# A streaming-encoder trunk on one core: entry in two row halves, half squares ahead of the last row tiles, weight sums first, and the up projections' stores on GpSimd's queue

## The chip, the core and the metric

The program runs on one core of a Trainium2 chip. The metric is the device time of one execution in microseconds (us). The core's engines are TensorE (PE, matrix products; its weight loads show as PEld), VectorE (DVE), ScalarE (ACT), GpSimd (POOL) and SyncE (SP, which only issues transfers here). Each engine takes its instructions in order. ACT and POOL can issue transfers too, and then the issue stands in their own order.

## The reference, cut to what matters

Two layers over 1024 rows of width 1024, all in float32. Layer 0 mixes with a gated short convolution, layer 1 with attention; both end in a squared-ReLU MLP of width 4096. Ahead of each mixer and MLP stands a norm, scaled and shifted by vectors that are made from the conditioning vector c.

```python
for l in range(DEPTH):
    mod = c_act @ ada_w[l] + ada_b[l]
    sh_m, sc_m, g_m, sh_f, sc_f, g_f = split(mod, 6)
    h = rmsnorm(x, norm_g[l, 0]) * (1 + sc_m) + sh_m
    y = short_conv_mixer(h, ...) if l < 1 else mla_mixer(h, ..., shared_kv(x, ...))
    x = x + g_m * rmsnorm(y, norm_g[l, 1])
    h = rmsnorm(x, norm_g[l, 2]) * (1 + sc_f) + sh_f
    y = square(relu(h @ mlp_up_w[l])) @ mlp_down_w[l]
    x = x + g_f * rmsnorm(y, norm_g[l, 3])

def short_conv_mixer(h, w_in, w_conv, b_conv, w_out):
    b_gate, c_gate, xh = split(h @ w_in, 3)
    return (b_gate * (causal_conv3(c_gate * xh, w_conv) + b_conv)) @ w_out
```

## The kernel before

The eight row tiles of 128 rows form two row halves (half 0, half 1), and the width of 1024 is eight blocks k of 128. Every float32 number is split into a high and a low part of a shorter type, and a product is three matmuls of 128 x 512 (low by high, high by high, high by low). Large products save one part in eight by seven products of sums of quarters (the names t1 to t4 and s in code and trace).

The stages in order: the **entry** (`conv_phase`: x is normed, scaled and transposed into k blocks, and the first two column blocks m=0, 1 of the convolution's input projection are made), three **triples** (the other column blocks in pairs, the convolution beside them), **down** (the convolution's output projection), the **first pairs** and the **up projection** of layer 0 (`mlp_up`, 16 pairs of column blocks; each pair's seven sums are stored to the DRAM arrays `ha`), **down_pairs** (reads `ha`, multiplies with the down weights, and at its end adds the residual row by row: the `Seam`), the latents, attention, and the same again for layer 1's MLP.

In the **entry**, pass 1 makes m=0 for both row halves, half 1 two k's behind (`LAG`); pass 2 makes m=1 with weights that are loaded again, 128 x 3 x 128 for each k. For each k, `ada` loads 128 columns each of shift and scale weights in four transfers, and DVE sums their eight 128 x 256 parts times c (`av`, L1006 and L1008); PE sums these over the partitions (L1010), ACT scales the transposed rows with the result (L1024), DVE makes the low part (L1025). The vectors' rows (norm gains, biases) are loaded by eight issues on ACT's queue ahead of ACT's first work.

In **down_pairs** the last product (number 2) leaves its last four k groups to the end and finishes them row tile by row tile (tiles 4 to 7). Each tile goes through `Seam.tile`: squares of the half that was ready before (L346), the add of the last half (L792), squares of it (L283), a root, the residual (L373), and where another stage follows, squares of the new row (L283), its scaling (L323) and a store. `seam.front` and `seam.back` interleave the next stage's h (`h_steps`: transposes on PE L482, ACT L485, DVE L491).

In the **up projection**, `pair_sums` makes the sums and splits of a pair's weights (L525 to L535) and `all_pairs` orders the products. `store` leaves the pair's row results, and `sums` (L1233 to L1238) makes seven stored operands of 128 x 512 and stores them, seven transfers of 256 KB, on ACT's queue. Row tiles come from a pool of eight; a pair takes four. A tile is free again when its stores have landed.

Within each engine most instructions stand in an order that a list scheduler made from the program's dependencies; what is written under `pinned` keeps the order of the code.

## Time and profile before

| | us |
|---|---|
| median of three runs | 2132.92 (2132.76 to 2133.66) |
| the profiled execution | 2132.76 |
| its span, first to last instruction | 2131.0 |
| entry, to the first product of the triples | 0 to 117.4 |
| layer 0: triples, down, first pairs, up | 117.4 to about 710 |
| layer 0: down_pairs, last tile's residual | to about 1033 |
| latents, attention, output projection, first pairs | to about 1536 |
| layer 1: up, down_pairs | to 2131 |

The mean granted clock of PE is 0.992 of full speed. The page's rows give an engine's busy time; a row of the timeline gives start, duration, engine, line, operation with its operands, how many were put together, and in brackets the idle time before it with the engine that ended it. A row of the windows gives start and end, length, then busy time and count of each engine, the granted clock, the DMA engines' share and GB/s. A row of the waits gives who waited for whom, the sum, how often, and the longest.

### The profile page before, as it was taken

The numbers are of one execution on the slowest core, as the hardware profiler recorded it, in microseconds if no ns is written. First come the engines' busy times: TensorE is split into PE (matmuls) and PEld (weight loads), VectorE is DVE, ScalarE is ACT, GpSimd is POOL, SyncE is SP. The second block draws the span as 40 slices with busy tenths as digits, with TensorE's granted clock in tenths as the row PEclk, the third lists the DMA queues.
The fourth block names the chain that finished last, engine by engine and source line by source line (L and its number), as shares of the span: only waits on it lengthen the run. The fifth ranks groups of instructions, "written<-read, shape, count | busy, mean of one in ns | idle before, by whom it ended". The sixth has DMA issues, their size and how long they took to land.

```text
span 2131.0 us, 25054 instructions
## 1 busy us (share of the span) xinstructions
PE 2054.8 (96%) x9438; PEld 1686.4 (79%) x9438; DVE 1553.8 (73%) x2100; ACT 1082.5 (51%) x1545; POOL 5.6 (0%) x13
## 2 busy tenths in 40 slices
PE   4999999999999999999899999999999999999998
PEld 3788878878888788888677788878878888888886
DVE  6877777886665579977688887758976765566577
ACT  4533354744454444455665565556745444544343
POOL 0000000000000000000000000000000000000000
PEclk9999999999999999999999999999999999999999
DMA  7344455355653889656223331135354653774255
GB/s 227 113 148 143 135 197 160 107 187 169 203 172 113 297 285 320 209 168 197 80 70 117 96 94 35 60 115 181 94 194 154 212 168 124 262 257 158 97 172 176
DMA packets 251166, 344.46 MB, mean 162 GB/s; under 512 B 19269, under 2 KB 142498, under 8 KB 251046
## 3 DMA queue, kind: packets, MB, share of 16 engines
q1 hardware_dynamic: 208840, 253.81, 37.9%
q10 hardware_dynamic: 42206, 89.06, 11.2%
q8 instruction: 74, 1.21, 0.2%
q14 instruction: 46, 0.38, 0.1%
HBM read 258.94 MB, written 83.89 MB: 161 GB/s over the span
## 4 chain that ended last, share of the span: by engine, by line
PE 78%; DVE 10%; ACT 5%; DMA 4%; issue 2%; SPq 0%; ACTq 0%; DVEq 0%
PE one L168 40%; PE mm L168 20%; PE big L168 7%; PE tp L168 6%; PE big L1471 2%; DMA raw<-ha 2%; DVE ring L172 1%; PE tp L1497 1%; ACT slot L1321 1%; DVE acc L198 1%; ACT junk L283 1%; ACT ring L171 1%; PE tp L421 1%; DVE raw L373 0%; DMA raw<-in_ada_w_dram 0%
## 5 line engine op out<-in xcount | busy, mean ns | idle before, releaser
L168 PE MATMUL one<-slot,uphi 128*128 128x512 f32 x1208 | 372.1, 389 | 0.0
L168 PE MATMUL one<-ring,ring 128*128 128x512 f32 x1152 | 262.9, 389 | 2.3 <-DVE ring L172 2.3
L168 PEld LDWEIGHTS one<-slot,uphi 128*128 128x128 f32 x1208 | 226.8, 188 | 47.2 <-issue 0.5
L168 PEld LDWEIGHTS one<-ring,ring 128*128 128x128 f32 x1152 | 215.9, 188 | 48.3 <-ACT ring L171 3.1
L168 PE MATMUL one<-slot,uplo 128*128 128x512 f32 x604 | 237.4, 393 | 5.2 <-DVE y L604 3.1
L172 DVE TENSOR_TENSOR uplo<-raw,uphi 128x1024 fp32r<-128x1024 f32 x129 | 157.6, 1222 | 85.5 <-ACT uphi L171 85.3
L172 DVE TENSOR_TENSOR ring<-raw,ring 128x1024 fp32r<-128x1024 f32 x144 | 174.2, 1219 | 59.0 <-ACT ring L171 58.6
L171 ACT ACTIVATE ring<-raw 128x1024 fp32r<-128x1024 f32 x144 | 149.4, 1052 | 120.0 <-DMA raw<-ha 76.6
L168 PE MATMUL mm<-ring,ring 128*128 128x512 f32 x768 | 185.1, 390 | 1.5 <-DVE ring L172 1.0
L168 PE MATMUL tp<-ring,ring 128*128 128x512 f32 x768 | 183.9, 389 | 0.0
L171 ACT ACTIVATE uphi<-raw 128x1024 fp32r<-128x1024 f32 x129 | 136.0, 1057 | 88.7 <-DVE raw L526 27.7
L168 PEld LDWEIGHTS mm<-ring,ring 128*128 128x128 f32 x768 | 143.6, 188 | 32.3 <-DVE ring L172 1.8
L168 PEld LDWEIGHTS tp<-ring,ring 128*128 128x128 f32 x768 | 144.1, 188 | 29.8
L171 ACT ACTIVATE ring<-w 128x1024 fp32r<-128x1024 f32 x80 | 84.7, 1059 | 158.8 <-PE tp L168 87.4
L172 DVE TENSOR_TENSOR ring<-w,ring 128x1024 fp32r<-128x1024 f32 x80 | 97.6, 1220 | 74.1 <-ACT ring L171 73.1
L198 DVE SCALAR_TENSOR_TENSOR acc<-raw,csil,acc 128x1024 f32<-128x1024 f32 x88 | 112.4, 1277 | 44.0 <-DMA raw<-in_ada_w_dram 39.3
L168 PEld LDWEIGHTS one<-slot,uplo 128*128 128x128 f32 x604 | 113.4, 188 | 32.4 <-DVE y L604 4.8
L168 PE MATMUL one<-slot,s 128*128 128x512 f32 x468 | 114.7, 395 | 6.3 <-DVE s L172 6.1
L168 PE MATMUL mm<-slot,uphi 128*128 128x512 f32 x360 | 110.9, 389 | 0.0
L168 PEld LDWEIGHTS one<-slot,s 128*128 128x128 f32 x468 | 88.6, 190 | 26.9 <-DVE s L172 7.4
L168 PE MATMUL one<-q,uphi 128*128 128x512 f32 x312 | 96.0, 389 | 0.0
L168 PE MATMUL big<-slot,slot 128*128 128x512 f32 x384 | 93.8, 391 | 1.8 <-ACT y L930 1.8
(283 smaller groups left out, 3566.0 us busy)
## 6 DMA issues: line engine op xcount, KB each, us to landing
ha<-y ACTq DMA_DIRECT2D x224, 256.0 KB, 2.4
raw<-ha SPq DMA_DIRECT2D x112, 512.0 KB, 4.4
raw<-in_ada_w_dram SPq DMA_DIRECT2D x80, 512.0 KB, 4.4
raw<-in_mlp_up_w_dram SPq DMA_DIRECT2D x72, 512.0 KB, 4.5
w<-in_mlp_down_w_dram SPq DMA_DIRECT2D x48, 512.0 KB, 6.0
raw<-in_mlp_down_w_dram SPq DMA_DIRECT2D x32, 512.0 KB, 4.0
xs<-raw ACTq DMA_DIRECT2D x19, 512.0 KB, 3.1
raw<-in_conv_in_w_dram SPq DMA_DIRECT2D x18, 512.0 KB, 4.0
```

Of the source, the lines that this page charges most:

```text
L168: nc.tensor.matmul(out_, lhs[a], rhs[b], start=first and i == 0, stop=last and i == 2, skip_group_check=more)
L171: nc.scalar.activation(hi, src, AF.Copy)
L172: nc.vector.tensor_tensor(lo, src, hi.bitcast(F32), op=ALU.subtract)
L198: nc.vector.scalar_tensor_tensor(acc, raw, s, acc, op0=ALU.mult, op1=ALU.add)
L283: nc.scalar.activation(junk[:, :src.shape[-1]], src, AF.Square, accum_out=ss)
L421: nc.tensor.transpose(p_[:, t * P:(t + 1) * P], ys[half * 4 + t][:, k * P:(k + 1) * P], ident)
L1321: nc.scalar.activation(y[32 * i:32 * i + 32, :], p_[32 * j:32 * j + 32, :], AF.Copy, scale=scale)
L1471: nc.tensor.matmul(o_, a, m_, start=j == 0, stop=j == 4)
L1497: nc.tensor.transpose(p_[:, c:c + P], pts[4 * hf + i][:, j * P:(j + 1) * P], ident)
```

## The change

Five things are changed.

1. **Entry.** Pass 1 now makes both column blocks of row half 0, pass 2 both of row half 1 (k in the order 0, 1, 4, 2, 5, 3, 6, 7). x's first half is loaded first. Modulation columns are loaded for k=0 and k=1 alone and then for two k's together (runs of 1 KB instead of 512 bytes; sums over 128 x 512). Weights are loaded once, 128 x 3 x 256 for each k, and their splits are kept for both passes. Only two of the vectors' loads stay ahead; the others follow x's second half on SP.
2. **Half squares.** The squares of the ready halves of row tiles 4 to 7 are taken together in the last product's pass, ahead of its last four groups; in the tile both products with the gain stand behind the add, tile 4 is treated like the others, and the next stage's piece is issued ahead of the tile.
3. **Weight sums.** For the pairs whose first products were made in the first pairs, and for the triples, `pair_sums` makes the sum s first, into a scratch of its own (in `mlp_up` the buffer "acc"), and the splits of a come before those of b. The next job's weights are loaded before `between`.
4. **First triple.** Its first pair of weights is loaded and split during the entry.
5. **Stores.** The 224 stores of `ha` are issued by `nc.gpsimd` instead of `nc.scalar`. The program gives the software queue `dynamic_dma_scratch_size=256`, before and after.

```diff
+    nc.scalar.dma_start(vrows[0:64, :], norm_g.rearrange("l v (k p) -> (l v k) p", p=P))
...
+    def later_rows():
...
+                       (kv_ada_b.rearrange("(k p) -> k p", p=P), 16)):
+            ld(mrows[r:r + n, :], src)
+            r += n
...
+        def half_squares(self, t, some):
+
+            junk = self.nx.tile([P, D], BF16, tag="junk", name=nm("junk"), bufs=1)
+            nc.scalar.activation(junk[:, HALF:], self.ys[t][:, HALF:], AF.Square, accum_out=some)
+            nc.vector.tensor_tensor(some, some, eps_d, op=ALU.add)
+            self.some[t] = some
...
-                if part:
-                    some = small()
-                    junk = self.nx.tile([P, D], BF16, tag="junk", name=nm("junk"), bufs=1)
-                    nc.scalar.activation(junk[:, HALF:], y[:, HALF:], AF.Square, accum_out=some)
-                    nc.vector.tensor_tensor(some, some, eps_d, op=ALU.add)
-                    gained(slice(HALF, D))
                 if add:
                     add()
                 if beside:
                     gained(slice(0, HALF if part else D))
-                else:
+                if part:
+                    gained(slice(HALF, D))
+                if part or not beside:
...
-    def pair_sums(up, a, b):
+    def pair_sums(up, a, b, s_=None):
...
-        nc.vector.tensor_tensor(a21, a21, a22, op=ALU.add)
-        yield
-        t2 = up_split(up, b)
-        yield
-        nc.vector.tensor_tensor(a21, a22, a11, op=ALU.subtract)
-        s2 = tuple(up.tile([P, 4, P], F32R, tag="s2" + "hl"[i], name=nm("s2"), bufs=1) for i in range(2))
-        split_w(s2[0], s2[1], a21)
-        nc.vector.tensor_tensor(a12, a12, a21, op=ALU.subtract)
-        yield {5: (t2, 0, "t1"), 4: (t2, 4, "t4"), 6: (s2, 0, "t2")}
-        t3 = up_split(up, a)
-        yield {7: (t3, 0, "t3"), 3: (t3, 4, "22")}
...
+        if s_ is None:
+            nc.vector.tensor_tensor(a21, a21, a22, op=ALU.add)
+            t2 = up_split(up, b)
+            nc.vector.tensor_tensor(a21, a22, a11, op=ALU.subtract)
+            split_w(s2[0], s2[1], a21)
+            nc.vector.tensor_tensor(a12, a12, a21, op=ALU.subtract)
+            yield
+            t3 = up_split(up, a)
+        else:
+            s_ = s_.rearrange("p (k m) -> p k m", k=4)
+            nc.vector.tensor_tensor(s_, a22, a11, op=ALU.subtract)
+            nc.scalar.activation(s2[0], s_, AF.Copy)
+            nc.vector.tensor_tensor(a12, a12, s_, op=ALU.subtract)
+            nc.vector.tensor_tensor(a21, a21, a22, op=ALU.add)
+            nc.vector.tensor_tensor(s2[1], s_, s2[0].bitcast(F32), op=ALU.subtract)
+            t3 = up_split(up, a)
+            yield
+            t2 = up_split(up, b)
+        yield {6: (s2, 0, "t2"), 7: (t3, 0, "t3"), 3: (t3, 4, "22"), 5: (t2, 0, "t1"), 4: (t2, 4, "t4")}
...
+    def half_acc():
+        return ad.tile([P, D], F32, tag="acc", name=nm("s_"), bufs=1)[:, :HALF]
...
-                ra, rb = raws()
+                ra, rb, *split = ready or raws()
...
+            ready = jobs[n + 1][0]() if n + 1 < len(jobs) else None
...
+                    if which == 2 and i == n - n_late - 1:
+                        with pinned():
+                            for t in range(4):
+                                seam.half_squares(4 + t, some[:, 8 * t:8 * t + 1])
...
-            seam.ahead, seam.beside = 4, 5
+            seam.ahead, seam.beside = 4, 4
             for t in range(4):
                 with pinned([mybir.EngineType.PE]):
                     for j, (pa, pb) in enumerate(late):
                         products(banks_[t], t, pa, pb, False, j == n_late - 1, True)
-                    seam.tile(4 + t, lambda: done(t, banks_[t]), [], False, True)
                     with pinned():
                         seam.front(steps, 1)
+                    seam.tile(4 + t, lambda: done(t, banks_[t]), [], False, True)
...
+        order = (0, 1, 4, 2, 5, 3, 6, 7)
...
+        def ada_sum(ks, raw):
+            acc = st.tile([P, 4 * P], F32, tag="av", name=nm("av"), bufs=2)[:, :len(ks) * 2 * P].rearrange("p (j m) -> p j m", j=2)
+            nc.vector.tensor_scalar(acc, raw[0], csil[:, 0:1], None, op0=ALU.mult)
+            for i in range(1, KD):
+                nc.vector.scalar_tensor_tensor(acc, raw[i], csil[:, i:i + 1], acc, op0=ALU.mult, op1=ALU.add)
+            for n, k in enumerate(ks):
+                sums_[k] = acc[:, :, n * P:(n + 1) * P]
...
+        def weights(k):
+
+            raw = ad.tile([P, D], F32, tag=("acc", "gmb")[k % 2], name=nm("w"), bufs=1)[:, :6 * P]
             ld(raw.rearrange("p (g m) -> p g m", g=3),
-               conv_in_w[0][k * P:(k + 1) * P, :].rearrange("p (g c) -> p g c", g=3)[:, :, m * P:(m + 1) * P])
-            w = [wr.tile([P, 3 * P], F32R, tag="w" + part_, name=nm("w"), bufs=4) for part_ in "hl"]
+               conv_in_w[0][k * P:(k + 1) * P, :].rearrange("p (g c) -> p g c", g=3)[:, :, :2 * P])
+            return raw
...
+            load_x(0)
+            wraws, sums_, ws, turned = [], {}, [], {}
+
+            def fetch(*ks):
+                raw = ada_cols(ks)
+                wraws.extend(weights(k) for k in ks)
+                return ks, raw
...
+            ada_sum(*aws[0])
+            turned[0] = turn(0, 0)
+            scales(0, lambda: ada_sum(*aws[1]))
+            turned[1] = turn(1, 0)
             acc = banks6()
-            for k in range(KD + LAG):
-                if k < KD - 1:
-                    w.append(weights(k + 1, 0))
-                    first_half(k + 1)
-                if k < KD:
-                    products(w[k], k, 0, acc)
-                if k == LAG:
+            for k in range(KD):
+                if k % 2 == 0 and k + 2 < KD:
+                    ada_sum(*fetch(k + 2, k + 3))
+                elif k + 2 == KD:
+                    load_x(1)
+                    later_rows()
+                products(ws[k], k, 0, 0, acc, k == 0, k == KD - 1)
+                if k + 1 < KD:
+                    scales(k + 1)
+                else:
+                    evict(0, 0, acc)
                     norm_x(1)
-                    second_half(0)
-                if k >= LAG:
-                    if k - LAG < KD - 1:
-                        second_half(k - LAG + 1)
-                    products(w[k - LAG], k - LAG, 1, acc)
-                if k == KD:
-                    w.append(weights(0, 1))
-            w = w[KD]
+                products(ws[k], k, 0, 1, acc, k == 0, k == KD - 1)
+                if k + 2 < KD:
+                    turned[k + 2] = turn(k + 2, 0)
...
+            for n, k in enumerate(order):
+                products(ws[k], k, 1, 0, acc, n == 0, n == KD - 1)
+                if len(ready) < KD:
+                    next_half()
+                elif n == KD - 2:
+                    feature_rows(mrows[:VEC_ROWS - 64 + 16, :], vecs[:, 64:VEC_ROWS], bias[:, 96:BIAS_ROWS])
+                products(ws[k], k, 1, 1, acc, n == 0, n == KD - 1)
+                if summed < 4 and summed in order[:n + 1] and summed + 4 in ready:
+                    sums(summed)
+                    summed += 1
+                if n == FIRST_KEPT - 1:
+                    wr.pop().release()
+                    up = pool("up", "right")
+                    begun = load_pair(conv_in_w[0], 4 + 1)
+                    begun += (up_split(up, begun[0]),)
...
-                nc.scalar.dma_start(ha[j][i], t_)
+                nc.gpsimd.dma_start(ha[j][i], t_)
```

Excerpts of the engines' orders at three places show where instructions went. First SP at the start of the entry (y is a row tile of x, aw the modulation columns, w the convolution's weights); before:

```order
L126 DMA craw<-in_c_dram 128x8x1
L126 DMA w_177<-in_conv_in_w_dram 128x3x128
L126 DMA aw_183<-in_ada_w_dram 128x4x128 x4
L126 DMA y_151<-in_x_dram 128x1024
L126 DMA y_152<-in_x_dram 128x1024
L126 DMA y_153<-in_x_dram 128x1024
L126 DMA y_154<-in_x_dram 128x1024
L126 DMA w_252<-in_conv_in_w_dram 128x3x128
L126 DMA aw_258<-in_ada_w_dram 128x4x128 x4
```

and after:

```order
L127 DMA craw<-in_c_dram 128x8x1
L127 DMA y_149<-in_x_dram 128x1024
L127 DMA y_150<-in_x_dram 128x1024
L127 DMA y_151<-in_x_dram 128x1024
L127 DMA y_152<-in_x_dram 128x1024
L127 DMA aw_171<-in_ada_w_dram 128x4x128 x4
L127 DMA w_176<-in_conv_in_w_dram 128x3x256
L127 DMA aw_178<-in_ada_w_dram 128x4x128 x4
L127 DMA w_183<-in_conv_in_w_dram 128x3x256
L127 DMA aw_271<-in_ada_w_dram 128x4x256 x2
```

x's four tiles moved to the head, the weights grew to both column blocks and stand behind the columns of their k. Then ACT at layer 0's last row tiles (y_5378 is tile 4 before, y_5310 after; raw and xr are residual rows); before:

```order
L283 ACTIVATE junk_7524,small_7525<-y_5378 128x1024
L285 ACTIVATE small_7527<-small_7525,eps_d 128x1
L283 ACTIVATE junk_7533,small_7534<-xr_7248 128x1024
L285 ACTIVATE small_7536<-small_7534,eps_d 128x1
L377 DMA xs_104<-xr_7248 128x1024
L485 ACTIVATE h_1020_7210<-one_7539,v_6818,v_6814 128x512
L485 ACTIVATE tt_7544<-one_7539,v_6818,v_6814 128x512
L346 ACTIVATE junk_7561,small_7560<-y_5379 128x512
L283 ACTIVATE junk_7567,small_7568<-y_5379 128x512
```

and after:

```order
L335 ACTIVATE junk_7367,some_6802<-y_5310 128x512
L335 ACTIVATE junk_7370,some_6802<-y_5311 128x512
L335 ACTIVATE junk_7373,some_6802<-y_5312 128x512
L335 ACTIVATE junk_7376,some_6802<-y_5313 128x512
L492 ACTIVATE h_1005_7143<-one_7414,v_6750,v_6746 128x512
L492 ACTIVATE tt_7419<-one_7414,v_6750,v_6746 128x512
L492 ACTIVATE h_1005_7143<-one_7422,v_6750,v_6746 128x512
L492 ACTIVATE tt_7427<-one_7422,v_6750,v_6746 128x512
L492 ACTIVATE h_1005_7143<-one_7462,v_6750,v_6746 128x512
L492 ACTIVATE tt_7467<-one_7462,v_6750,v_6746 128x512
L287 ACTIVATE junk_7481,small_7482<-y_5310 128x512
```

The four half squares now stand together, before three pieces of h, and tile 4's own squares are of half a row. At the start of layer 0's up projection, DVE before (the L172 that makes s is the weight sum's low part, L530 makes the sum, L1234 to L1236 the stored operands of the pair before):

```order
L615 TENSOR_TENSOR y_3346<-y_3346,mm_3430 128x512
L525 TENSOR_TENSOR raw_3562<-raw_3562,raw_3564 128x512
L526 TENSOR_TENSOR raw_3564<-raw_3564 128x512
L1234 TENSOR_TENSOR y_3098<-y_3098,y_3345 128x512
L172 TENSOR_TENSOR uplo_3465<-raw_3459,uphi_3464 128x1024
L1235 TENSOR_TENSOR y_3417<-y_3098 128x512
L530 TENSOR_TENSOR raw_3459<-raw_3459,raw_3457 128x512
L1236 TENSOR_TENSOR y_3418<-y_3345,y_3417 128x512
L533 TENSOR_TENSOR raw_3457<-raw_3457,raw_3459 128x512
L624 TENSOR_TENSOR y_3100<-y_3100,one_3395 128x512
L630 TENSOR_TENSOR y_3346<-y_3346,mm_3430 128x512
L172 TENSOR_TENSOR s_592_3470<-raw_3459,s_591_3469 128x512
```

and after, where L544 makes the sum and L548 its low part:

```order
L606 TENSOR_TENSOR y_3325<-y_3029,one_3324 128x512
L544 TENSOR_TENSOR s__571_3392<-raw_3349,raw_3347 128x512
L618 TENSOR_TENSOR y_3325<-y_3325,mm_3364 128x512
L1297 TENSOR_TENSOR y_3027<-y_3027,y_3274 128x512
L546 TENSOR_TENSOR raw_3347<-raw_3347,s__571_3392 128x512
L1298 TENSOR_TENSOR y_3351<-y_3027 128x512
L547 TENSOR_TENSOR raw_3349<-raw_3349 128x512
L1299 TENSOR_TENSOR y_3352<-y_3274,y_3351 128x512
L548 TENSOR_TENSOR s_573_3394<-s__571_3392,s_572_3393 128x512
L176 TENSOR_TENSOR uplo_3402<-raw_3347,uphi_3401 128x1024
```

The sum is made one operation behind L606 and needs no split of b; six operations of 128 x 512 stand between it and its low part, where ten with a split of 128 x 1024 among them stood between L615 and the low part before. On POOL, whose queue held no transfer before, the second pair's stores now stand so (acc_4263 is cleared for the gate's vector of a later stage):

```order
L1301 DMA ha_101<-y_3029 128x512
L1301 DMA ha_106<-y_3457 128x512
L1301 DMA ha_102<-y_3325 128x512
L1301 DMA ha_103<-y_3325 128x512
L1301 DMA ha_104<-y_3029 128x512
L1301 DMA ha_105<-y_3457 128x512
L188 MEMSET acc_4263 128x1024
L1301 DMA ha_107<-y_3458 128x512
```

Behind six stores a clearing stands in the queue, and the seventh store behind it.

218 lines of the change are left out of this document (107 added, 111 removed).

## The prediction

> **What bounds the kernel now.** I read the page first, for the engine that is busy most.
>
> ```profile
> PE 2054.8 (96%) x9438; PEld 1686.4 (79%) x9438; DVE 1553.8 (73%) x2100; ACT 1082.5 (51%) x1545; POOL 5.6 (0%) x13
> ```
>
> PE is busy for 2054.8 of 2131.0 us, so at most 76 us of idle time can be won, and a little time at a reduced clock; the number of products stays what it was. Next come the windows, cut where PE has gaps and where it has none.
>
> ```profile
> core 0: us, PE busy (x) PEld busy (x) DVE busy (x) ACT busy (x) POOL busy (x), PEclk, DMA share, GB/s
> 0.00:25.00 25.00, 5.26 (x18) 3.46 (x18) 14.37 (x42) 11.02 (x20) 1.48 (x9) 1.00 1.00 294
> 25.00:60.00 35.00, 26.99 (x121) 21.94 (x121) 26.40 (x65) 19.04 (x33) 0.00 (x0) 0.85 0.64 173
> 430.00:460.00 30.00, 25.72 (x111) 20.32 (x110) 25.21 (x36) 14.87 (x17) 0.00 (x0) 1.00 0.59 194
> 460.00:680.00 220.00, 220.00 (x968) 181.28 (x967) 147.81 (x191) 109.22 (x137) 0.00 (x0) 1.00 0.52 170
> 1005.00:1037.00 32.00, 25.33 (x105) 19.71 (x104) 16.05 (x29) 21.17 (x43) 0.00 (x0) 0.84 0.22 82
> 2100.00:2131.00 31.00, 22.35 (x97) 17.56 (x95) 19.24 (x28) 8.99 (x21) 0.00 (x0) 0.94 0.35 125
> ```
>
> The idle time sits in four places: the first 60 us (27.8 us), the start of an up projection (4.3 us), the seam behind layer 0's down projection (6.7 us) and the very end. In an up projection's steady part (460 to 680) PE is never idle: nothing that frees another engine can gain there, but something that becomes slower than PE can lose.
>
> **The entry.** The timeline of PE gives its landmarks, and the groups by line and form what DVE and ACT pay.
>
> ```profile
> 25.08 2.91 PE L168 MATMUL mm<-slot,w 128*128 128x512 f32 x6
> 39.24 0.98 PE L1010 MATMUL tp<-ones,av 128*128 128x1 f32 x4 [6.86 <-DVE av L1008]
> 40.09 2.91 PE L168 MATMUL mm<-slot,w 128*128 128x512 f32 x6
> 54.80 0.60 PE L1018 MATMUL tp<-cs,y 128*128 128x128 f32 x4
> 102.47 2.88 PE L168 MATMUL one<-slot,w 128*128 128x512 f32 x12
> 105.19 1.52 PE L168 MATMUL mm<-slot,w 128*128 128x512 f32 x6
> 117.43 0.39 PE L168 MATMUL one<-slot,uplo 128*128 128x512 f32 x1
> ```
> ```profile
> L1008 DVE SCALAR_TENSOR_TENSOR av<-aw,csil,av 128x256 f32<-128x256 f32 x56 | 26.6, 481 | 1.0
> L172 DVE TENSOR_TENSOR w<-w,w 128x384 fp32r<-128x384 f32 x16 | 8.8, 552 | 1.7 <-ACT w L171 1.7
> L1083 DVE TENSOR_SCALAR y<-y,small 128x1024 f32<-128x1024 f32 x8 | 6.0, 749 | 0.1
> L1024 ACT ACTIVATE q<-tp,sh 128x512 f32<-128x512 f32 x8 | 6.2, 769 | 0.0
> L1025 DVE TENSOR_TENSOR slot<-q,slot 128x512 fp32r<-128x512 f32 x8 | 5.5, 688 | 3.9 <-ACT q L1024 3.9
> L198 DVE SCALAR_TENSOR_TENSOR acc<-raw,csil,acc 128x1024 f32<-128x1024 f32 x3 | 3.8, 1279 | 0.8 <-DMA raw<-in_ada_w_dram 0.8
> ```
>
> Products begin at 25.08, lose 6.86 us at 39.24, and run at half speed behind both (six take 2.91 us, at full speed 1.52). The entry ends at 117.43. Twelve products are 2.72 us apart (102.47 to 105.19), so one k of one row half with both column blocks, 18 products, costs 4.08 us.
>
> The start: the first 25 us move 294 GB/s. What k=0 needs is now 2.1 MB of x, 1.05 MB of modulation columns and 0.4 MB of weights, 3.5 MB, at that rate some 12 to 14 us. DVE then does four norms (0.75 each, paced by ACT's squares) and eight sums of 0.48, to about 17.3; the modulation's matmuls, ACT's two scalings (0.77 each) and the low part (0.69) give first products at about 20.5 instead of 25.1.
>
> Row half 0 has 8 x 4.08 = 32.6 us of products, and DVE is the slower there. A paired sum over 512 columns lies between 481 ns (256) and 1279 ns (1024); by the straight line it is 0.75, so eight of them are 6.0 per two k. With the low part (0.69), a weight split of twice the columns (0.55 to 1.1, taken 0.96) and two small operations (0.37), DVE needs 3.0 + 2.0 = 5.0 us for a k, against PE's 4.08. Its work from 12.4 to the last low part is 16 sums of 0.48 for the two single k's, 18 us for three pairs, 16 us of the rest and 3.6 us for the norms of x's second half, which stand ahead of k=7: about 60. The last k's products end the half at about 65. Row half 1 starts about 2.5 us later (two transposes, a scaling, a low part) and has 32.6 us of products with six groups of four transposes inside (0.60 at 54.80): 104. **The entry gains 13.4 us.** If a 512-column sum costs 0.6, PE leads and it is 18; if PE's short waits bring the half speed of 40.09 back for some 5 us, it is 8. The weights' second load, 1.6 MB, goes; ACT's eight early issues become three, and six short loads go behind x's second half on SP.
>
> **The up projections' starts.** Here the timeline shows ACT and its issues.
>
> ```profile
> 435.37 5.59 ACTq L1238 DMA_DIRECT2D ha<-y  x5
> 441.00 0.63 ACT L171 ACTIVATE s<-raw 128x512 fp32r<-128x512 f32 x1 [4.72 <-DVE y L1236]
> 443.05 3.02 PE L168 MATMUL one<-slot,s 128*128 128x512 f32 x12 [2.73 <-DVE s L172]
> 457.18 2.88 PE L168 MATMUL one<-slot,s 128*128 128x512 f32 x12
> 459.90 0.39 PE L168 MATMUL one<-q,uplo 128*128 128x512 f32 x1
> 1553.81 4.61 PE L168 MATMUL one<-slot,s 128*128 128x512 f32 x12 [2.73 <-DVE s L172]
> ```
>
> ACT stands in its store issues from 435.37 to 440.96, and the weight sum's high part behind them comes at 441.00: PE waits 2.73 us, in both layers, and the second time twelve products also take 4.61 instead of 3.02. With the stores off ACT's queue and the sum ahead of the splits, the high part can run at about 436 and the low part, behind six DVE operations of 0.69, at about 440.3, when PE comes to it. **Gain 2 x 2.73 + 1.6 = 7.1**, between 5 (a rest of the wait stays) and 9 (shorter waits of 0.78 for the first product's sum go too; they hang on a DVE result that the change does not move, so I keep them).
>
> The 224 stores themselves now are POOL's. Their bound is PE's pair: seven products of 12 matmuls, 7 x 2.72 = 19.04 us (457.18 to 459.90 is one), for seven stores of 256 KB.
>
> ```profile
> ha<-y ACTq DMA_DIRECT2D x224, 256.0 KB, 2.4
> ACT s L171 <- DMA ha<-y: 50.3, 14, 4.0
> POOL acc L184 <- DVE raw L373: 678.1, 2, 389.0
> ```
>
> From issue to landing a store takes 2.4 us today. If POOL handled them strictly one after the other at that price, seven would be 16.8 us, within 19.04, so I take nothing for them; no row shows a store from POOL, so the price is open from 0 up to whatever a descriptor written in software costs. The ACT waits of 50.3 us go, but PE did not wait for them in the steady part. POOL's clearing of acc now stands between two stores of the second pair and holds what is behind it until that buffer, now a weight sum's scratch, is free; about one store waits. The Trainium skill's page "DMA: Bandwidth & Descriptors", section "Anatomy of one DMA — SWDGE (gpsimd) path", fits such a transfer as 2.0 us plus its bytes over 436 GB/s. By that fit a store would be an estimated 2.6 us and seven 18.2: still inside the pair, so the sum would stand, but with 0.8 us to spare instead of 2.2, and the first rival below would be the likelier for it; no run here shows it yet.
>
> **The seam behind layer 0's down projection.**
>
> ```profile
> 1005.78 0.68 DVE L792 TENSOR_TENSOR y<-y,mm 128x512 f32<-128x512 f32 x1
> 1026.81 1.22 PE L168 MATMUL big<-h,uphi 128*128 128x512 f32 x2 [5.43 <-DVE h L491]
> 1035.10 1.15 ACT L323 ACTIVATE y<-raw,small 128x1024 f32<-128x1024 f32 x1 [0.23 <-DVE small L290]
> 1035.88 0.76 PE L482 MATMUL tp<-cs,y 128*128 128x128 f32 x4
> 995.00:1005.00 10.00, 10.00 (x54) 8.47 (x53) 3.00 (x4) 5.43 (x8) 0.00 (x0) 1.00 0.51 162
> 2080.00:2090.00 10.00, 10.00 (x46) 8.29 (x45) 9.34 (x9) 3.56 (x4) 0.00 (x0) 1.00 0.69 235
> ```
>
> The chain of four row tiles runs from 1005.78 to the last scaled row at 1036.25, and half 1's transposes wait for it; on the way PE waits 5.43 us for an h that stands behind a tile. After the change the front's piece goes ahead of each tile, the half squares are gone from it, and both products with the gain stand behind the add. ACT then has per tile a half square (1.1 with its root), a full one (1.5), two h pieces (1.55) and the scaling (1.14): about 5.4, with a wait for DVE some 5.7, and 6.5 pass from a tile's add to its scaled row (0.7, 1.1, 1.5, 1.5, 1.2 and the hand-overs), so the fourth tile's row is ready at 1005.8 + 3 x 5.7 + 6.5 = 1029.4. **Gain 6.3**, between 4 and 8. The four half squares (0.63 and a read of 0.19 each) move into the pass before, where ACT has 4.6 of 10 us free (6.4 of 10 in layer 1) and PE no gap; without that cover they would cost 3.3 us.
>
> **The end.**
>
> ```profile
> 2112.32 11.04 PE L168 MATMUL tp<-ring,ring 128*128 128x512 f32 x48
> 2122.86 0.63 ACT L346 ACTIVATE junk<-y 128x512 bf16<-128x512 f32 x1 [1.94 <-DVE raw L373]
> 2124.30 0.68 DVE L792 TENSOR_TENSOR y<-y,tp 128x512 f32<-128x512 f32 x1
> ```
>
> PE ends at 2123.36, the last add starts at 2124.30 behind a half square that waited for the tile before. Now it can start at about 2123.5, but both gain products (0.69) follow before the last step: **0.5 gained**, between 0 and 0.8. The stretch from 117 to 425, where one pair's loads now come ahead, I leave at zero, give or take 1.
>
> **The sum.** 13.4 + 7.1 + 6.3 + 0.5 = 27.3. The profiled execution took 2132.76 (its span 2131.0 and 1.8 around it), beside the median of 2132.92: 2132.8 - 27.3 = 2105.5.
>
> **The rivals.** First, slower than before: **POOL's stores do not keep up.** For it speaks that nothing is known of their rate here and that the program gives that queue's descriptors only 256 bytes a partition, so that a store may wait for the one before; against it, 2.4 us today against 2.72 allowed. Above 2.72 us a store POOL is the slower engine, and with some 15 us of slack from the row buffers (eight tiles, four a pair) PE stalls: at 3.0 us a pair is 21.0, 2.0 more, 16 pairs 31, less 15: 16 a layer, 32 in all, 2138, a loss. At 3.5 it is 5.5 x 16 - 15 = 73 a layer, 2251. The gain is gone from about 2.95 us on. One rule of the Trainium skill would make this the outcome: the page "SBUF — State Buffer", section "Who interferes with whom", has descriptors from GpSimd wait while DVE holds a port pair that the two share. It names copies and tensor_scalar as the operations that hold it and infers that tensor_tensor leaves the writing free. DVE is busy for 147.81 of 220 us there, two thirds; if each of its operations locked POOL out, 2.4 us would become 7, 49 us a pair. But by the groups of that stretch DVE runs only forms with two tensor inputs:
>
> ```profile
> L172 DVE TENSOR_TENSOR uplo<-raw,uphi 128x1024 fp32r<-128x1024 f32 x35 | 42.8, 1223 | 30.7 <-ACT uphi L171 30.7
> ```
>
> so by the page's letter it does not bite. The whole rival gets 0.20.
>
> Second, **the entry stays bound by DVE and its loads**: a paired sum that costs twice a single one (0.96) adds 1.7 us a pair, the loads of k=6 and 7 wait for buffers that these sums hold, and the half speed returns. It gains 3 to 5 instead of 13: 2114 to 2116. For it speaks that 5.0 is already over 4.08; chance 0.15.
>
> Third, **the starts and the seam keep their waits**: DVE takes its rows in order, so the weight sum's low part and h can still come late by what is queued ahead. Then only the entry and a third of the rest remain: 2114; chance 0.08.
>
> **The numbers.** The forecast, 2105.5, with its own range of 2094 to 2112, has 0.55; the remaining 0.02 lies below it. The range is 2094 to 2130: it takes in both smaller gains, and leaves out most of the slow stores (0.17) and the 0.02. A measurement of this kernel can tell about 0.2%, 4.3 us, from no change. Faster by more has 0.79, since of the slow stores a little lies here too; within 4.3 us 0.05; slower 0.16.
>
> **What would show it.** Right: first products at 20 to 21, no wait near 7 us in the entry, the first product of the triples at 102 to 106; twelve s products without a wait at the starts; transposes of half 1 at about 1029 on the old clock; POOL's issues of a pair done in under 19 us. Wrong: PE waiting in the steady up part for a row buffer that a store holds, PE's share of 460 to 680 under 100%, or gaps of several us between the products of row half 0.

## The result, and the profile after

| | median us | runs | range |
|---|---|---|---|
| before | 2132.84 | 4 | 2130.52 to 2133.66 |
| after | 2210.02 | 4 | 2208.03 to 2212.45 |

The ratio is 1.0364, with a 95% interval of 1.0346 to 1.0382: the changed kernel is slower by 77 us, where a gain of 27 was forecast. The profiled execution's span is 2210.4 us.

The page of after answers first, by its busy times, and by its groups and DMA issues (busy time and mean ns, then idle time before and its releaser; for issues KB and us to landing):

```profile
PE 2081.1 (94%) x9439; PEld 1696.2 (77%) x9439; DVE 1543.3 (70%) x2074; ACT 1077.5 (49%) x1542; POOL 127.6 (6%) x237
L1301 POOL DMA_DIRECT2D ha<-y x224 | 122.3, 546 | 1346.7 <-ACT y L1289 764.1
ha<-y POOLq DMA_DIRECT2D x224, 256.0 KB, 2.3
```

PE is busy 26 us longer for the same products, some of them at a lower clock (the granted clock is 0.983 on the mean, 0.992 before). The other part of the loss is idle: 129.3 us in place of 76.2. A store of ha takes 2.3 us from issue to landing, no longer than before. The price of one store, as a latency, was forecast well; the loss hides behind that line. The windows show where it is:

```profile
core 0: us, PE busy (x) PEld busy (x) DVE busy (x) ACT busy (x) POOL busy (x), PEclk, DMA share, GB/s
420.00:460.00 40.00, 35.23 (x146) 28.07 (x146) 31.89 (x47) 20.51 (x23) 8.75 (x15) 0.96 0.37 125
460.00:700.00 240.00, 221.91 (x941) 178.17 (x940) 136.69 (x178) 101.65 (x132) 41.44 (x76) 0.98 0.46 150
700.00:760.00 60.00, 50.92 (x214) 40.86 (x213) 24.01 (x26) 23.03 (x26) 8.95 (x17) 0.94 0.55 203
```

PE now waits in the middle of an up projection, where it was never idle before (220.00 of 220), and on into the start of the down projection (700 to 760). No engine is busier for it. The list of waits names what they wait for (us in total, times, longest):

```profile
POOL ha L1301 <- issue: 329.3, 122, 6.2
ACT y L584 <- DMA ha<-y: 186.4, 22, 11.3
ACT ring L175 <- DMA raw<-ha: 111.5, 36, 18.0
DVE y L1296 <- DMA ha<-y: 73.1, 24, 6.5
PE one L172 <- DVE y L618: 36.2, 12, 7.3
```

ACT and DVE wait for row buffers y until the stores have read them, PE then waits for DVE; and POOL, with stores to issue, waits 122 times for nothing that the profile shows. POOL's timeline shows how it goes:

```profile
557.29 0.54 POOL L1301 DMA_DIRECT2D ha<-y  x1 [2.06 <-ACT y L1285]
559.89 0.54 POOL L1301 DMA_DIRECT2D ha<-y  x1 [2.05 <-issue]
562.50 0.55 POOL L1301 DMA_DIRECT2D ha<-y  x1 [2.06 <-issue]
565.12 0.54 POOL L1301 DMA_DIRECT2D ha<-y  x1 [2.08 <-DVE y L1297]
570.48 0.54 POOL L1301 DMA_DIRECT2D ha<-y  x1 [4.82 <-issue]
```

A store is issued every 2.60 us, whatever the releaser named, and one after 5.36. The trace's packets, worked out store by store from its records (80 packets each), show why:

```
issue   first packet  last packet  packets' time   next issue
559.89     561.00       561.84         0.84          562.50
562.50     563.61       564.47         0.87          565.12
565.12     566.26       569.90         3.64          570.48
570.48     571.60       572.44         0.84          573.09
```

Each issue comes about 0.65 us behind the last packet of the store before, and in none of the 224 stores less than 0.58 us behind it: two are never under way together. Of 2.60 us the packets move for 0.84. The third store meets SP's loads, whose issues stand here, and its packets take 3.64:

```profile
563.61 2.08 SPq L127 DMA_DIRECT2D raw<-in_ada_w_dram  x2
```

Three rows of the timelines of DVE, ACT and PE show what hangs on it:

```profile
570.30 0.69 DVE L1299 TENSOR_TENSOR y<-y,y 128x512 f32<-128x512 f32 x1 [4.38 <-DMA ha<-y]
572.89 0.60 ACT L584 ACTIVATE y<-one 128x512 f32<-128x512 f32 x1 [10.59 <-DMA ha<-y]
572.84 0.50 PE L172 MATMUL one<-q,uplo 128*128 128x512 f32 x1 [3.02 <-DVE y L618]
```

DVE's row starts behind that store's last packet (569.90) and landing (570.18), and PE loses 3.02 us behind it. The other parts of the change do what was said. PE's timeline of the entry:

```profile
21.55 3.73 PE L172 MATMUL one<-slot,w 128*128 128x512 f32 x8 [0.76 <-DVE slot L1043]
65.33 1.53 PE L172 MATMUL mm<-slot,w 128*128 128x512 f32 x6
105.42 0.39 PE L172 MATMUL one<-slot,uplo 128*128 128x512 f32 x1
```

First products at 21.55 (25.08 before), row half 0 done at 66.86, the triples at 105.42 (117.43 before). So the question is narrow: the stores, and why seven of them do not fit where they seemed to.

### The profile page after: what moved, and what is told of

The parts are those of the page before. It is cut to its first block, busy times and chain, and to the rows that moved or that the text cites. A ratio compares the mean times of both kernels' runs of the same rounds, so it can differ in the third digit from the quotient of the medians.

```text
span 2210.4 us, 25183 instructions
## 1 busy us (share of the span) xinstructions
PE 2081.1 (94%) x9439; PEld 1696.2 (77%) x9439; DVE 1543.3 (70%) x2074; ACT 1077.5 (49%) x1542; POOL 127.6 (6%) x237
## 4 chain that ended last, share of the span: by engine, by line
issue 51%; PE 31%; DMA 6%; DVE 5%; ACT 3%; POOL 3%; SPq 0%; POOLq 0%; DVEq 0%; ACTq 0%
PE one L172 16%; PE mm L172 6%; PE big L172 4%; PE tp L172 3%; POOL ha L1301 3%; DMA ha<-y 2%; DMA raw<-in_ada_w_dram 1%; ACT uphi L175 1%; DVE ring L176 1%; DMA raw<-ha 1%; ACT y L1285 1%; DVE y L591 0%; DMA raw<-in_conv_out_w_dram 0%; DVE uplo L176 0%; DMA w<-in_conv_in_w_dram 0%
## 5 line engine op out<-in xcount | busy, mean ns | idle before, releaser
L172 PE MATMUL one<-slot,uphi 128*128 128x512 f32 x1208 | 373.6, 391 | 0.0
L172 PE MATMUL one<-ring,ring 128*128 128x512 f32 x1152 | 272.0, 398 | 20.7 <-DVE ring L176 14.1
L172 PEld LDWEIGHTS one<-ring,ring 128*128 128x128 f32 x1152 | 220.5, 192 | 71.2 <-ACT ring L175 11.8
L172 PEld LDWEIGHTS one<-slot,uphi 128*128 128x128 f32 x1208 | 227.7, 188 | 47.4 <-issue 0.5
L172 PE MATMUL one<-slot,uplo 128*128 128x512 f32 x604 | 239.6, 397 | 18.5 <-ACT y L604 15.2
L1301 POOL DMA_DIRECT2D ha<-y x224 | 122.3, 546 | 1346.7 <-ACT y L1289 764.1
L172 PE MATMUL mm<-ring,ring 128*128 128x512 f32 x768 | 185.0, 390 | 1.2 <-DVE ring L176 1.2
L172 PE MATMUL tp<-ring,ring 128*128 128x512 f32 x768 | 183.9, 389 | 0.0
L175 ACT ACTIVATE uphi<-raw 128x1024 fp32r<-128x1024 f32 x129 | 135.8, 1057 | 90.1 <-PE one L172 31.2
L172 PEld LDWEIGHTS mm<-ring,ring 128*128 128x128 f32 x768 | 143.7, 188 | 31.7 <-DVE ring L176 2.1
L172 PEld LDWEIGHTS tp<-ring,ring 128*128 128x128 f32 x768 | 144.1, 188 | 29.8
L172 PEld LDWEIGHTS one<-slot,uplo 128*128 128x128 f32 x604 | 113.9, 189 | 50.6 <-ACT y L604 22.3
L172 PE MATMUL one<-slot,s 128*128 128x512 f32 x468 | 116.6, 399 | 5.7 <-DVE s L548 5.5
L584 ACT ACTIVATE y<-one 128x512 f32<-128x512 f32 x33 | 19.8, 598 | 203.6 <-DMA ha<-y 186.4
L172 PE MATMUL mm<-slot,uphi 128*128 128x512 f32 x360 | 111.0, 389 | 0.0
L172 PEld LDWEIGHTS one<-slot,s 128*128 128x128 f32 x468 | 90.3, 194 | 26.6 <-DVE s L548 7.4
```

The source lines that it names most:

```text
L172: nc.tensor.matmul(out_, lhs[a], rhs[b], start=first and i == 0, stop=last and i == 2, skip_group_check=more)
L175: nc.scalar.activation(hi, src, AF.Copy)
L584: nc.scalar.activation(a[:, :HALF], x_, AF.Copy)
L1301: nc.gpsimd.dma_start(ha[j][i], t_)
```

## The experiments

Times are medians beside runs of before on the same chip (2131.58 us for the first four, 2134.22 for the fifth to eighth, 2131.93 to 2133.5 for the rest); differences between experiments on different chips carry that much uncertainty. "Behind" means by how much PE reaches the product of the same number later than in another kernel's trace, worked out from its records; "by position" means such a number.

**1. The stores back on ScalarE.**

```
-                nc.gpsimd.dma_start(ha[j][i], t_)
+                nc.scalar.dma_start(ha[j][i], t_)
```

> The changed kernel with one word undone: the 224 stores of ha go back to ACT's queue. Theory T (the software queue holds one store of 256 KB at a time, so that seven of them, 2.6 us each and more where loads share the DMA engines, no longer fit the 19.04 us of a pair on PE): the whole loss goes, about 2105 us, with PE busy in the up projections' steady part as before. Theory O (the new order of weight sums and the scratch in the buffer acc cause the waits, whichever queue the stores take): stays above 2190.

2106.96 us, ratio 0.9883 (0.9867 to 0.99). Without the moved stores the rest of the change gains 24.6 us. The window of its up projection is full again:

```profile
460.00:680.00 220.00, 219.96 (x967) 181.09 (x966) 139.21 (x179) 105.73 (x134) 0.00 (x0) 1.00 0.51 167
```

**2. More room for GpSimd's descriptors.**

```
-    ... dynamic_dma_scratch_size=256)
+    ... dynamic_dma_scratch_size=512)
```

> The changed kernel with the software queue's descriptor space doubled, 512 bytes a partition instead of 256; the stores stay on GpSimd's queue. Theory T (one store in flight because of the space): up to three stores in flight, POOL's issues follow each other in about 1 us instead of 2.6, the row buffers come free in time, and the time falls to 2100 to 2110. Theory S (writing the descriptors in software takes 2.6 us a store whatever the space): stays at 2205 to 2215. Theory O: stays above 2190.

2102.74 us, ratio 0.9863 (0.9848 to 0.9877): changing one number takes away 107.3 us, with every store still on GpSimd. It is the fastest kernel of the study, ahead of the kernels before and after. POOL's timeline, its windows and its DMA issues:

```profile
540.91 1.67 POOL L1301 DMA_DIRECT2D ha<-y  x3 [5.28 <-ACT y L1288]
543.54 0.55 POOL L1301 DMA_DIRECT2D ha<-y  x1 [0.96 <-DVE y L1297]
```
```profile
420.00:460.00 40.00, 39.22 (x174) 32.14 (x173) 36.31 (x53) 23.17 (x27) 13.03 (x23) 1.00 0.70 225
460.00:700.00 240.00, 238.16 (x1046) 195.67 (x1045) 148.08 (x190) 118.89 (x150) 47.25 (x88) 1.00 0.54 179
700.00:760.00 60.00, 60.00 (x266) 49.71 (x265) 37.18 (x34) 23.39 (x25) 1.44 (x3) 1.00 0.75 261
```
```profile
ha<-y POOLq DMA_DIRECT2D x224, 256.0 KB, 3.2
PE 2046.2 (97%) x9439; PEld 1681.6 (80%) x9439; DVE 1544.9 (74%) x2074; ACT 1082.8 (52%) x1542; POOL 126.7 (6%) x237
```

Three stores leave without a pause, 0.55 us each, and the next 2.63 us after the first of them. POOL's waits for nothing that the profile shows fall from 329.3 us to 30.2. A single store now takes 3.2 us to land, 0.9 longer than in the slow kernel: what changed is how many are under way. The spans differ by 110.4; 34.9 of it is PE's busy time (2081.1 against 2046.2; the granted clock was 0.94 to 0.98 in after's windows above, and 1.00 here), 75.5 is idle.

**3. Room between the two (384).** This kernel ran once.

> As the run with 512 bytes, but 384: half as much again as the changed kernel has. Theory T: two stores in flight if a store takes nine descriptors an engine, so most of the loss goes, 2100 to 2125. Theory S: 2205 to 2215.

2114.85 us. POOL's issues come in twos:

```profile
545.89 1.08 POOL L1301 DMA_DIRECT2D ha<-y  x2 [5.37 <-ACT y L1288]
548.54 0.54 POOL L1301 DMA_DIRECT2D ha<-y  x1 [1.57 <-DVE y L1297]
```

PE is busy for all of 460 to 680, so two under way are enough there. In the same stretch it makes 956 products where experiment 2 makes 969, and it was already later in the entry, before the first store (106.53 for the triples against 105.10). The 12 us to experiment 2 are thus mostly not waits for stores. Its products themselves start farther apart: 229.8 ns on the mean between 500 and 600 us, where experiment 2 has 226.7, which makes 19.30 us a pair in place of 19.04, at a granted clock of 1.00 in both. What slows them stays open.

**4. The stores' move alone.** The kernel before, with nothing but its stores on GpSimd.

```
-                nc.scalar.dma_start(ha[j][i], t_)
+                nc.gpsimd.dma_start(ha[j][i], t_)
```

> The kernel before with one word changed: its 224 stores of ha issued from GpSimd's queue with 256 bytes of descriptor space; entry, half squares and weight sums stay old. Theories T and S: the loss of the stores alone, 2133 + about 95 to 110 = 2228 to 2243. Theory O: within 5 us of 2133.

2226.3 us, ratio 1.0449 (1.0433 to 1.0464): this edit alone costs 94.7 us, without any other part of the change. The time lies just under the range that was expected.

**5 and 6. Fewer of the seven stores on GpSimd**, in every pair, at 256: all but the first in 5, and all but the first two in 6 (`j < 2`).

```
-                nc.gpsimd.dma_start(ha[j][i], t_)
+                (nc.scalar if j < 1 else nc.gpsimd).dma_start(ha[j][i], t_)
```

> The changed kernel (256 bytes) with one of a pair's seven stores, the first, on ACT's queue and six on GpSimd's. In the changed kernel's trace a store takes 2.6 us alone, and two of seven meet loads and take some 2.4 us more, 23.5 us a pair. Theory L (loads that share the DMA engines lengthen two stores a pair in any case): 6 x 2.6 + 2 x 2.4 = 20.4 us a pair, still over 19.04, so PE keeps some waits, about 2108 to 2125. Theory J (the long stores come only of the jam itself; a pair needs 18.2 us otherwise): 15.6 us, no wait, 2101 to 2106.

> As the run with six, but two of seven stores (the first two) on ACT's queue and five on GpSimd's. Theory L: 5 x 2.6 + 2 x 2.4 = 17.8 us a pair, within 19.04, so the loss is gone: 2101 to 2107. Theory J: the same. A third reading, that any use of the software queue with 256 bytes stalls PE: above 2125.

Six: 2122.03 us, ratio 0.9942 (0.9927 to 0.9957). Five: 2104.58, ratio 0.9858 (0.9843 to 0.9873). With six GpSimd's queue still costs 19.3 us against experiment 2 by the medians and 16.9 by the ratios. With five PE loses nothing to experiment 2 by position in either up projection: the loss is not spread over the stores but begins at a number per pair. Experiment 5 is a miss of theory J, by which only the jam itself makes long stores; experiment 6 fits both theories.

**7, 8 and 9. The other parts, one undone at a time**, each at 512, so beside 2102.74: the second product's weight sum in its old order; the half squares back in the seam's row tiles; the old entry with its early row loads.

```
-   lambda begun: None if begun is None else half_acc(), [lambda: store(0, ca[0], cb), finish])
+   lambda begun: None, [lambda: store(0, ca[0], cb), finish])
```
```
+                if part:
+                    some = small()
...
-                    ss = squares(self.nx, y[:, :HALF], self.some[t])
+                    ss = squares(self.nx, y[:, :HALF], some)
...
-            seam.ahead, seam.beside = 4, 4
+            seam.ahead, seam.beside = 4, 5
```

> The changed kernel with 512 bytes, and in the up projections the old order of the weight sums (split of b first, the sum in place). It asks whether the starts gain by the sum being first or by ACT's queue being free of stores. If the order gains it, about 8 us over the 512-byte run, 2108 to 2113, with waits near 2.7 us at both starts; if the freed queue does, within 2 us of it, 2101 to 2105; between if each does a part.

> The changed kernel with 512 bytes, and the half squares, the products with the gain and the next stage's piece put back into the row tiles as before the change. By the prediction's terms it loses 6.3 us at layer 0's seam and 0.5 to 1 at the end: 2109 to 2111 beside 2102.7 for the 512-byte run, with PE's wait of about 5.4 us for h back. If the seam's gain came with the other parts: within 2 us of 2102.7.

> The changed kernel with 512 bytes and the entry of before (both row halves in pass 1, single columns, weights loaded twice, all vector rows ahead on ACT's queue, the first triple's pair not begun in it); all other parts stay changed. By the prediction's term the entry is worth 13.4 us, by the traces so far 12.3: 2114 to 2117 beside 2102.7 for the 512-byte run. If the entry's gain were given back later, by the later loads, less than 6 us: under 2109.

Old sum order 2110.83 us (8.1 slower; by position 2.9 at each of the two starts of the up projections). Old half squares 2110.91 (8.2 slower; by position 7.1 at the seam, 0.8 at the end). Old entry 2115.28 (12.5 slower). The first two ran on another chip than experiment 2; by the ratios to before they are 4.7 and 5.1 slower.

**10 and 11. Without the loads of the modulation that run beside the stores** in the up projections (they come later instead), at 256 and at 512; layer 1's call is changed in the same way.

```
-    last = mlp_up(0, up, hs, firsts, 2)
+    last = mlp_up(0, up, hs, firsts, 0)
```

> The changed kernel (256 bytes, seven stores on GpSimd's queue) without the modulation work beside the up projections' pairs, so that their two loads of 512 KB a pair are gone there; the same work follows behind the last pair. To be read against its twin with 512 bytes. Theory L (a store that meets loads takes some 2.4 us more, one at a time): 7 x 2.6 + about 2.4 = 20.6 us a pair against 19.04, so only 10 to 30 us over the twin, where the changed kernel is 107 over its own. Theory J (the stores jam by themselves): still 70 or more over the twin.

> The same with 512 bytes of descriptor space, the twin of the run without loads. The modulation work, about 16 sums a layer of 1.28 us on DVE with their loads, then stands behind the last pair; both theories: no store wait, and 2103 to 2140 by what of that work shows at the start of the down projection.

2203.34 us and 2113.56: the loss is still 89.8 us, where the theory of the loads said 10 to 30. The loads of the modulation thus fall as the main cause. The other loads are not excluded: SP still loads the up projection's weights beside the stores, and the stores' time hardly fell. In the steady part POOL now needs 20.6 us a pair (565.13, 585.68 and 606.33 are one store of three pairs), still over PE's 19.04, and over the fifteen steps of layer 0 22.0 us a pair (22.3 in after).

**12 and 13. The first four pairs apart.** Each of these pairs needs fewer products, since two were made before the stage; experiment 12 takes their stores off GpSimd, 13 (the two engines swapped) leaves only theirs there.

```
-                nc.gpsimd.dma_start(ha[j][i], t_)
+                (nc.scalar if i < AHEAD else nc.gpsimd).dma_start(ha[j][i], t_)
```

> The changed kernel (256 bytes); the stores of the first four pairs of each up projection on ACT's queue, those of the other twelve on GpSimd's. Theory F (the backlog is made by the first four pairs, five products or 13.6 us each for seven stores of 2.6, and uses up the row buffers' slack before the steady part begins): most of the loss goes, 2110 to 2135. Theory L alone (stores that meet loads, in every pair): the first four count no more than others, 2175 to 2195.

> The reverse: the stores of the first four pairs on GpSimd's queue, the other twelve pairs' on ACT's. Theory F with its price by the changed kernel's own trace (6 to 9 us of PE lost per layer by the fourth pair, later pairs then free): 2115 to 2125. Theory F as the whole cause (the start alone makes the loss): above 2160. Theory L alone: 2125 to 2135, a quarter of the loss.

2161.52 us, ratio 1.0133 (1.0118 to 1.0148), and 2133.97, ratio 1.0003 (0.9994 to 1.0013). Experiment 12 lies between the ranges of the two theories and is a miss of both. Experiment 13 lies between the two forms of the theory that blames the first four pairs (2115 to 2125 with the later pairs free, above 2160 if they made the whole loss), a miss of both. By its number it is in the range of the loads (a quarter of the stores, a quarter of the loss); but that theory missed 10 and 12, so one number that fits doesn't save it. What the two say together: taken off, they give back 48.5 us; left alone, they cost 31.2. The 17 between is what their backlog does to the pairs behind them. In 13, PE is 16.1 us behind experiment 2 at 500 us of layer 0 and stays so until the stage is over. In 12 it is 4.3 behind at 600, 15.3 at 690 and 29.8 at 740. Two rows of PE's timeline there, the second in the down projection, which reads ha:

```profile
697.88 0.79 PE L172 MATMUL one<-q,uplo 128*128 128x512 f32 x1 [6.89 <-DVE y L618]
...
747.16 8.00 PE L172 MATMUL one<-ring,ring 128*128 128x512 f32 x23 [3.54 <-DVE ring L176]
```

**14. The last four pairs as well.** Only pairs 4 to 11 stay on GpSimd.

```
-                nc.gpsimd.dma_start(ha[j][i], t_)
+                (nc.scalar if (i < AHEAD or i >= 12) else nc.gpsimd).dma_start(ha[j][i], t_)
```

> The changed kernel, with the stores of the first four and of the last four pairs of each up projection issued from ScalarE, and only those of pairs 4 to 11 from GpSimd. With the first four pairs alone on ScalarE 2161.5 us were measured, and by the positions of equal products TensorE then falls behind by about 4 us in the middle of the first up projection, by 11 in its last pairs and by 14.5 at the start of the down projection. Theory B (backlog): the last two losses come from stores that still stand in GpSimd's queue when the last pairs' tiles and the down projection's reads of ha want them; with the last four pairs on ScalarE both go, the 4 us of the middle stay, per layer: 2105 to 2120 us, and TensorE's waits for VectorE of about 7 us near 698 us are gone. Theory S (sharing): the last losses come from the transfers themselves, whichever queue issued them, or from the pairs before; then the time stays at 2145 to 2162 us.

2131.3 us, ratio 0.9988 (0.9978 to 0.9998): 30.2 less than experiment 12, and between the two theories' ranges: a miss of both. Its rows of PE:

```profile
657.55 0.80 PE L172 MATMUL one<-slot,uplo 128*128 128x512 f32 x1 [6.91 <-ACT y L604]
...
709.02 51.22 PE L172 MATMUL one<-ring,ring 128*128 128x512 f32 x224 [1.15 <-DVE ring L176]
```

The start of the down projection runs through, so its 14.5 us were backlog in front of its reads. A loss of 10.1 us stays, earlier now: about 650 us, while the stores of the last of the eight pairs are issued (639.62 to 658.09).

## Why the prediction was wrong

**The step that failed** is in the part on the up projections' starts: "seven would be 16.8 us, within 19.04, so I take nothing for them". The term was 0; it measured 107.3 us (experiment 2 against after). Both sides of that comparison were off, and the choice of value with them.

*The stores' side.* That POOL handles them strictly one after the other held. But the time from issue to landing isn't the period: behind a landing at 2.3 us another 0.3 pass, so 2.60 undisturbed, 18.2 a pair. By the fit of the Trainium skill's page "DMA: Bandwidth & Descriptors", section "Anatomy of one DMA — SWDGE (gpsimd) path", a store was an estimated 2.6 us, and the trace's period agrees. On top of that come stores that meet loads, which the sum didn't have at all. The first store of each pair in after, and in experiment 2 until pair 9 (POOL's issues, every seventh):

```
pair                 0       1       2       3       4       5   ...   9      15
after             421.98  443.22  465.24  488.69  509.52  530.38  625.19  757.15
experiment 2      421.56  432.84  445.64  459.10  477.96  497.00  573.16
```

The stores of a pair take 21.9 us on the mean of the first four, 22.3 on all fifteen steps (757.15 - 421.98 = 335.2), where I had 16.8. The packets split the 335.2: 105 stores at 2.60 are 273.0, and of the 62.2 above that 57.5 are in 29 stores that took over 0.25 us longer than the others from issue to last packet. During 22 of these 29, with 52.6 of the 57.5 us, packets of SP's loads moved too. At 273.0 the stores would be only 7 us behind PE's 265.8 below, within a slack of 15. By this account, which no run without any loads confirms, one store at a time and the loads that it meets make the loss together.

*PE's side.* In experiment 2, where stores don't bind, a pair takes 19.04 us only from pair 4 on. The first four take 56.4 together, 14.1 each, since two of their seven products are done by then; they have all seven stores. The quoted steady window showed the budget of twelve pairs of sixteen, and I used it for all. Even 7 x 2.60 = 18.2 is over 14.1, though for four pairs that alone is 16.4 us, about the slack.

**The first rival had the mechanism.** It took the stores' time of the stage less PE's, less some 15 us of slack from the row buffers, per layer. With the measured numbers:

```
                        stores' time   PE's time     over   less 15   measured a layer
all pairs (after)           335.2        265.8       69.4      54       107.3 / 2 = 53.7
first four (13)              87.5         56.4       31.1      16        31.2 / 2 = 15.6
pairs 4 to 11 (14)          182.7        152.3       30.4      15        28.6 / 2 = 14.3
```

(PE's time is 56.4, 477.96 - 421.56, and 19.04 for each pair behind it; the 87.5 is from after's rows; the 182.7 is eight times the mean of seven steps in experiment 14, 479.77 to 639.62.) All three agree within 2 us with times measured on the chip. But the stores' times were read after the fact, and the 15 us of slack are the prediction's figure, which no run measures by itself. On other runs the formula does less well: a layer of experiment 12 gives 28.6 against 29.4 measured, of experiment 10 49.6 against 44.9, of experiment 5 18.3 against 9.6. So the loss is the backlog of one queue whose rate is below PE's, sized by this to within some 9 us a layer. The slack is paid once: that is why the first four pairs cost 31.2 alone but 48.5 in company. The steps of 12, 14 and 2 divide the 107.3 into 48.5 (first four), 30.2 (last four) and 28.6 (the middle); that they add up is no test, since each starts where the one before ends. The thresholds of 5 and 6 fit too: six stores are 15.6 us undisturbed, over 14.1, five are 13.0.

So the mechanism stood there as a rival with 0.20, and with the right question ("a store may wait for the one before"). What sent it under was the budget of 19.04 against 2.4 a store. The rival's "gain is gone from about 2.95 us on" (2.98 by its own terms) was too kind as well, since it too counted 19.04 for all sixteen pairs: at 335.2 / 105 = 3.19 us a store its formula gives some 38 a layer, where 53.7 were measured. With 14.1 for the first four the gain would be gone from an estimated 2.80 on.

The port rule of the Trainium skill's page "SBUF — State Buffer", section "Who interferes with whom", shows no part in it: POOL's record of a store is 546 ns on the mean in after, with DVE busy 136.69 of 240 us beside it, and 543 in experiment 2, with DVE busy 148.08 of 240 us. What POOL waits for goes when the room for descriptors grows.

**The other terms held, the starts with more than their range**, by experiment 2's trace and the single parts undone:

| term | forecast | measured |
|---|---|---|
| entry | 13.4 | 12.3 (117.43 to 105.10); 12.5 by experiment 9 |
| starts of the up projections | 7.1, 5 to 9 | 9.8 by position (4.1 and 5.7); of it the old order gives back 5.8 (experiment 7), the stores on ACT 2.5 (1 against 2) |
| seam | 6.3, 4 to 8 | 7.1 by position; 7.1 by experiment 8 |
| end | 0.5 | 0.4 from 2090 us on; 1.0 behind the last product (8.00 to 7.00) |
| all | 27.3 | 28.8 by medians (2131.58 to 2102.74), 31.0 by spans (2131.0 to 2100.0) |

The entry's landmarks came at 21.55, 66.86 and 105.42 where 20.5, 65 and 104 stood, and no wait near 7 us is left in it. The 2.73 us for the weight sum go in experiments 1 and 2, but not in after, where DVE has by then lost 3.24 and 1.67 us to row buffers that stores still read:

```profile
441.67 4.53 PE L172 MATMUL one<-slot,s 128*128 128x512 f32 x12 [2.95 <-DVE s L548]
```

The clearing of acc between two stores, which I put at about one store waits, takes 0.97 us in layer 0 by POOL's timeline, and the store behind it starts 2.60 us after the one ahead, as any other:

```profile
456.84 0.97 POOL L188 MEMSET acc<- 128x1024 f32 x1
458.90 0.54 POOL L1301 DMA_DIRECT2D ha<-y  x1 [1.09 <-DVE y L1298]
```

Left open: why experiment 3's products are slower than experiment 2's, and how much time the loads as a whole cost. By the packets they make most of what a pair takes beyond 18.2 us, but that is read from one trace. Experiment 10 took one kind of them away and the loss fell from 107.3 to 89.8; those of the weights were not tried.

## What to carry to other kernels

A transfer's time from issue to landing says nothing of how many a queue takes per time: before work moves to another queue, ask how many can be under way there, and multiply the period, not the latency. Make the budget for each part of a stage, its start above all, where fewer products may stand beside the same number of transfers; and add up backlog over the stage, less the buffers' slack once. When a queue that is hardly busy (6% here) makes others wait, look for what it waits for before an issue, and raise that limit before the work is moved back.

## What the runs showed of the hardware

- GpSimd's stores of 256 KB with 256 bytes a partition for its descriptors: one under way, issues 2.60 us apart, the next issue about 0.65 us behind the last packet. With 384 bytes at most two of the 224 were under way together, with 512 at most three, and the kernel goes from 2210.0 to 2102.7 us.
- Such a store is 1.11 us from issue to first packet (559.89 to 561.00) and 0.84 us of packets; beside SP's loads the packets took up to 3.64 us, and with one store under way the next issue came nearly that much later (5.36 us in place of 2.60).
- With more under way each store lands later (3.2 us against 2.3), and the kernel is 4.9% faster.
